# Dealing tokens to blocks by runs of 32, and two steps put elsewhere in the queues

## The chip, the cores and the metric

The kernel runs on one core of one Trainium2 chip. The metric is the device time of one execution in microseconds (us). "PE" is the TensorE matmul engine (PEld its weight load), DVE is VectorE, ACT is ScalarE, POOL is GpSimd, SP is SyncE, which here only issues DMAs.

## The reference

One layer of a decoder trunk over 512 tokens with 1024 channels, in float32: a SwiGLU feed-forward, a mixer (a gated linear recurrence beside attention in a window of 128 with sinks), and a second feed-forward. Each has a norm on its input and a norm on its output before the residual sum.

```python
def swiglu(x, w_gu, w_down):
    gate, up = jnp.split(x @ w_gu, 2, axis=-1)
    return (jax.nn.silu(gate) * up) @ w_down
...
x = x + 0.5 * rms_norm(swiglu(rms_norm(x, ffn1_pre_g[l]), ffn1_w_gu[l], ffn1_w_down[l]), ffn1_post_g[l])
y = hybrid_mixer(rms_norm(x, mix_pre_g[l]), ...)
x = x + rms_norm(y, mix_post_g[l])
x = x + 0.5 * rms_norm(swiglu(rms_norm(x, ffn2_pre_g[l]), ffn2_w_gu[l], ffn2_w_down[l]), ffn2_post_g[l])
```

The feed-forwards have 2816 hidden channels, 22 chunks of 128.

## The kernel before

**Arithmetic.** Every float32 operand of a product is split into a high part in PE's reduced float32 (`float32r`, rounded by a copy on ACT) and a low part (the rest, a subtraction on DVE). A product is three matmuls: high by high, high by low, low by high. For weights as for activations, DVE makes the low parts, and so PE waits for DVE where a low part is late.

**Seven products for eight.** In most groups the product of a 2x2 block matrix is made from seven block products instead of eight, with sums and differences of blocks on DVE ahead of them. The forms of the left operand are made by `Next.sums` and `Next.lows` (normed input, four calls for each feed-forward, kept for all groups of chunks). The hidden activations' forms for the down product are made by `seven_left` and `seven_right`: a11, s3, a12, s2, s4, a22, s1, in the order in which `seven_down` multiplies them.

**First feed-forward.** Chunks 0 to 3 are made by the plain path (`classic`) with a plain down product; then four groups of four chunks (4-7, 8-11, 12-15, 16-19) run in `octo`, and the last two chunks in `quad`. `octo` multiplies with tokens as the output's partitions, so the 512 tokens are dealt to four blocks of 128 (`NB` = 4). Block b gets tokens b, b + 4, b + 8 and so on: in `sums`, the product of x, gain and the inverse norm reads `xT` and `R` with a step of four words and writes a block as one run. The result of `octo` is turned back by DVE's 32x32 transposes (`turned`, line 934), which write `z` with a step of four words, so that `z` has the tokens in their natural order; `put` writes `z` to HBM by the queue of SP, and `fetch` brings it back with channels as partitions. `quad` with `dealt` set (the last pair of chunks) writes its high and low parts with the same step (lines 862 and 865).

While group g runs in `octo`, the forms of group g - 1 are made beside it (`seven_forms_of`), and after it `seven_down` makes the down product of g - 1, so there are three of these here, for chunks 4-7, 8-11 and 12-15. The second feed-forward has three `seven_down` too (chunks 6-9, 10-13, 14-17), with `quad` and no dealing.

**The order on the engines** is the order of the program: each engine has one queue, written out by hand. `W.take` hands out a weight tile and lets ACT and DVE split units ahead of it; a raw weight buffer whose units are all split is loaded anew. `hid.steps` is a list of small DVE and ACT steps, of which `seven_down` does one behind each product. In the first feed-forward the first of them has been done in `octo` already; so the steps stand one product earlier there than in the second.

**The residual stream.** `xT`, two tiles of 1 MB, lies in two of the five buffers for raw weights. In the first group, behind the down product's fourth chunk (c = 3), `lend` copies both tiles to HBM (POOL's queue, line 1305) and `W.load(2)` has SP load the next two raw weights into buffers that this frees. Later `give_back` fetches the stream. The down product's chunks are staged by ACT (line 1365) and put to HBM by POOL (line 1366).

**Tile buffers.** `wt` has 8 buffers and `t2k` 38; a new tile takes the buffer that was freed first, in program order, and waits for its last reader.

Of the kernel before, what the change touches and what calls it, by code (L numbers as in the profile page):

```python
# [12 lines left out]
ALU = mybir.AluOpType  # L13
AX = mybir.AxisListType

P = 128
T = 512
NB = T // P
# [101 lines left out]
def tile_layer(ctx: ExitStack, tc: tile.TileContext, out: bass.AP, **ins: bass.AP):  # L120
    nc = tc.nc
    pe, dve, act, pool, sync = nc.tensor, nc.vector, nc.scalar, nc.gpsimd, nc.sync
# [12 lines left out]
    HALF = [slice(0, T // 2), slice(T // 2, T)]  # L135
# [23 lines left out]
    def wt(name, w=T, dt=F32):  # L159
        return tmp.tile([P, w], dt, tag="w", name=name, bufs=NW)  # L160


    W = Weights()
# [378 lines left out]
    def stream():  # L542

        xs = [wpool.tile([P, 4 * T], F32, tag="raw", name=f"xT{i}", bufs=NRAW) for i in range(2)]
        return xs, [x[:, c * T:(c + 1) * T] for x in xs for c in range(4)]

    x_tiles, xT = stream()
# [8 lines left out]
    def x_low(x, src, gain, sl):  # L556
        dve.scalar_tensor_tensor(x[1][:, sl], src, gain, x[0].bitcast(F32)[:, sl], op0=ALU.mult, op1=ALU.subtract)

    class Next:


# [35 lines left out]
        def sums(self, k):  # L597


            n = f"{self.name}{k}"  # L600
            xa, xb, t13, t24 = (wt(f"{s}_{n}") for s in ("xa", "xb", "ta", "tb"))
            some = (lambda nm, dt: spare.pop() if spare else t2k(nm, dt)) if self.name != "a" else t2k
            if self.name != "a" and k < 2:
                spare.extend(fours(f"sums{k}", F32R))
            b11 = some(f"b11_{n}", F32R)
            highs = [some(f"{s}h_{n}", F32R) for s in ("b2", "t13", "t24")]
            l, r = HALF
            dealt = (lambda t: t.rearrange("p (t b) -> p b t", b=NB)) if self.dealt else lambda t: t
            for x, c in ((xa, k), (xb, k + 4)):
                dve.scalar_tensor_tensor(x.rearrange("p (b t) -> p b t", b=NB) if self.dealt else x, dealt(xT[c]), self.gain(c), dealt(self.R), op0=ALU.mult, op1=ALU.mult)  # L610
            act.copy(b11[:, l], xa[:, l])
            dve.tensor_sub(t13[:, l], xa[:, r], xa[:, l])
            dve.tensor_sub(t13[:, r], xb[:, r], xa[:, r])
            dve.tensor_sub(t24[:, l], xb[:, r], t13[:, l])
            dve.tensor_sub(t24[:, r], xb[:, l], t24[:, l])
            for h, x in zip(highs, (xb, t13, t24)):
                act.copy(h, x)
            self.made = n, xa, b11, highs, (xb, t13, t24)
# [147 lines left out]
    class Hidden:  # L766
# [45 lines left out]
        def seven_right(self, f, x, second):  # L812

            self.blocks[second, 1] = x
            a11, a21 = self.blocks[0, 0], self.blocks[0, 1]
            if not second:
                s3 = wt(f"s3{self.name}{f}")
                dve.tensor_sub(s3, a11, a21)
                self.form("s3", s3)
                return  # L820
            a12, a22 = self.blocks[1, 0], x
            s1, s2, s4 = (wt(f"{s}{self.name}{f}") for s in ("s1", "s2", "s4"))
            dve.tensor_sub(s1, a22, a21)
            dve.scalar_tensor_tensor(s2, s1, -1.0, a11, op0=ALU.mult, op1=ALU.subtract)

            for name, y in (("a22", a22), ("s1", s1), ("s2", s2)):
                W.later(1, self.high, name, y)

            def last_sum():
                dve.scalar_tensor_tensor(s4, s2, -1.0, a12, op0=ALU.mult, op1=ALU.subtract)  # L830
                self.high("s4", s4)
                self.low("s1")

            self.steps = [lambda: self.low("s2"), last_sum, lambda: self.low("s4"), lambda: self.low("a22")]

        def quad(self, f, last, ahead, seven_down=False, beside=lambda i: None):

            n = f"{self.name}{f}"
            l, r = HALF
            hs = None if seven_down else [(t2k(f"hh{n}{j}", F32R), t2k(f"hl{n}{j}", F32R)) for j in range(2)]  # L840

            def seven(b, form, first, ahead=AHEAD):
                hi, lo = W.take(ahead)
                for j in range(2):
                    o, js = b[:, HALF[j]], slice(j * P, (j + 1) * P)
                    for k in range(4):
                        xh, xl = self.nxt.t[form, k]
                        for i, (w, x) in enumerate(((hi, xh), (hi, xl), (lo, xh))):
                            pe.matmul(o, w[:, k, js], x, start=first and i + j + k == 0, stop=k == 3 and i == 2, skip_group_check=True)  # L849

            def low_parts(x, h):
                if seven_down:
                    (self.seven_right if h else self.seven_left)(f, x, last)
                    return
                def own(t):
                    return t.rearrange("p (t b) -> p b t", b=NB)[:, 2 * h:2 * h + 2] if self.nxt.dealt else t[:, HALF[h]]

                def like(t):
                    return t.rearrange("p (b t) -> p b t", b=2) if self.nxt.dealt else t

                for j in range(2):
                    act.copy(own(hs[j][0]), like(x[:, HALF[j]]))
                for j in range(2):
                    hh, hl = hs[j]
                    dve.tensor_sub(own(hl), like(x[:, HALF[j]]), own(hh.bitcast(F32)))  # L865

            def last_half():
                dve.tensor_mul(g1, g1, u4)

            A, D, B = (bank(f"{s}{n}") for s in "adb")  # L870
            p1, p7, u4 = (wt(f"{s}{n}") for s in ("p1", "p7", "u4"))
            u2, g1 = ((t2k if seven_down else wt)(f"{s}{n}") for s in ("u2", "g1"))
            seven(A, "b11", True)
            act.copy(B, A)
            seven(D, "t3", True)
            act.copy(p7, D)
            beside(1)
            seven(A, "t2", False)
            act.copy(u2, A)
            beside(2)  # L880
            seven(B, "b21", False)
            W.later(1, act.activation, p1, B, AF.Silu)
            beside(3)
            seven(A, "t1", False)
            act.copy(u4, A)
            beside(4)
            W.later(1, dve.tensor_add, u4, p7, u4)
            seven(D, "t4", False)
            dve.tensor_add(u2, u2, D)
            dve.tensor_mul(u2, p1, u2)  # L890
            W.later(1, low_parts, u2, 0)
            beside(5)
            seven(A, "b22", False, ahead)
            act.activation(g1, A, AF.Silu)
            if last:
                last_half()
                low_parts(g1, 1)
            else:
                W.later(1, last_half)
                W.later(2, low_parts, g1, 1)  # L900
            if not seven_down:
                for j in range(2):
                    self.hs[f + j] = hs[j]

        def octo(self, f, beside):


            n = f"{self.name}{f}"
# [22 lines left out]
            def turned(xs, h):  # L931

                for tb, x in enumerate(xs):
                    dve.transpose(z.rearrange("p (j n b) -> p b j n", n=32, b=NB)[:, 2 * h + tb], x.rearrange("p (j n) -> p j n", n=32))  # L934

                def put():
                    for i in range(4):
                        sync.dma_start(h_hbm[:, i * P:(i + 1) * P].rearrange("(j a) n -> a j n", a=32), z[32 * i:32 * (i + 1)].rearrange("p (j n) -> p j n", n=P))

                if h:  # L940
                    W.later(1, put)
# [4 lines left out]
            z = wide(f"z{n}")  # L946
# [355 lines left out]
    def lend(tiles):  # L1302

        for x, h in zip(tiles, xT_hbm):
            pool.dma_start(h, x)
# [9 lines left out]
    for g, (f0, f1) in enumerate(GROUPS1):  # L1315
# [18 lines left out]
        for c in range(KD):  # L1334
# [25 lines left out]
            b = pair_banks[c] if c < 2 else product(W.take(), xs, name=f"ya{g}{c}")  # L1360
            if g == 0 and c in (0, 1, 3, 4):
                (n1.sums if c in (0, 3) else n1.lows)(2 + c // 3)
            if g == 0:
                st = t2k("stage")
                act.activation(st, b, AF.Copy, scale=-1.0 if c >= KD // 2 else 1.0)
                pool.dma_start(in_hbm[c // 2][:, :, c % 2], in_halves(st))
                if c == 3:
                    lend(x_tiles)
                    W.load(2)
            else:  # L1370
                res.chunk(c, b, parts[c])

# [81 lines left out]
    for j in range(4):  # L1454
        b = in_product(f"pq{j}")
# [401 lines left out]
    for i in range(2):  # L1857
        x = wpool.tile([P, 2 * D], F32, tag="raw", name=f"x_rows{i}", bufs=NRAW)
# [82 lines left out]
```

## Time and profile before

| | us |
|---|---|
| median of 3 runs | 866.05 (864.41 to 869.21) |
| the profiled execution | 867.49 |
| its span, first to last instruction | 865.8 |
| PE busy | 850.1 |
| DVE busy | 717.8 |
| ACT busy | 520.1 |
| POOL busy | 212.1 |

In the profiled execution, group 4-7 begins in `octo` at 79 us; the three `seven_down` of the first feed-forward begin at 157, 221 and 280 us, those of the second at 659, 718 and 778 us. Times in rows are counted from the span's start. Matmuls are pipelined: one of 512 columns is shown as 0.39 us and the next starts 0.23 us later, so for PE a stretch's length between two products says more than the busy time of single rows.

### The profile page before, as it was taken

How to read it: one execution, taken by the hardware profiler on the slowest of the kernel's cores; microseconds unless marked ns; L12 is line 12 of the kernel's file. 1: busy time of each engine (PE TensorE's matmuls, PEld its weight loads, DVE VectorE, ACT ScalarE, POOL GpSimd, SP SyncE). 2: the span in 40 equal slices, each digit the busy share in tenths (PEclk: the TensorE clock that was granted, in tenths of full speed). 3: DMA queues.
4: the chain of work that ended last, by engine and by line, in shares of the span. 5: the costliest groups of instructions: out<-in, count | busy, mean ns of one | idle time of the engine just before them, and what ended most of it. 6: DMA issues, size and time to landing. Idle time of an engine off the chain costs nothing.

```text
span 865.8 us, 13808 instructions
## 1 busy us (share of the span) xinstructions
PE 850.1 (98%) x5252; PEld 764.0 (88%) x5252; DVE 717.8 (83%) x984; ACT 520.1 (60%) x871; POOL 212.1 (25%) x228
## 2 busy tenths in 40 slices
PE   9999999899999999999999999999999999999996
PEld 8988788798988998998788899888999998998995
DVE  4988898978979866889989589788789798889856
ACT  6645746476576565466888446444656666658552
POOL 2012000050230244344556045110201402303502
PEclk9999999999999999999999999999999999999999
DMA  7248419298396699322211140267733955938922
GB/s 245 75 149 291 161 55 309 72 240 279 81 254 212 137 254 328 109 69 78 98 50 50 49 137 11 65 144 229 263 97 103 235 156 132 234 98 184 261 91 97
DMA packets 118914, 133.85 MB, mean 155 GB/s; under 512 B 23152, under 2 KB 85952, under 8 KB 118336
## 3 DMA queue, kind: packets, MB, share of 16 engines
q1 hardware_dynamic: 103504, 98.23, 36.1%
q0 software_dynamic: 15200, 34.61, 17.9%
q8 instruction: 41, 0.67, 0.3%
q14 instruction: 25, 0.20, 0.1%
q10 hardware_dynamic: 144, 0.13, 0.0%
HBM read 96.25 MB, written 36.70 MB: 154 GB/s over the span
## 4 chain that ended last, share of the span: by engine, by line
PE 69%; DVE 15%; DMA 6%; issue 4%; ACT 4%; POOL 2%; SPq 1%; DVEq 0%; ACTq 0%; POOLq 0%
PE ab L849 11%; PE db L849 5%; PE aa L924 4%; PE bb L849 3%; PE da L924 2%; DMA raw_ad__3208<-in_ffn_w_down 2%; PE ba L924 2%; DVE za L934 2%; PE yb L1801 1%; PE yb L1800 1%; PE yb L1802 1%; PE wo L1755 1%; DMA raw_ayd__1426<-in_ffn_w_down 1%; DMA raw_ay__902<-in_ffn_w_gu 1%; PE yab L1824 1%
## 5 line engine op out<-in xcount | busy, mean ns | idle before, releaser
L1072 POOL DMA_DIRECT2D yp_a<-stage x42 | 36.3, 1053 | 188.3 <-ACT stage L1069 177.6
L1072 POOL DMA_DIRECT2D yp_b<-stage x42 | 36.8, 1145 | 148.8 <-ACT stage L1069 140.9
L480 PE MATMUL ya<-hla,whi_ad 128*128 128x512 f32 x62 | 24.2, 391 | 0.2 <-DVE hla L865 0.2
L479 PE MATMUL ya<-hha,whi_ad 128*128 128x512 f32 x62 | 24.1, 389 | 0.0
L481 PE MATMUL ya<-hha,wlo_ad 128*128 128x512 f32 x62 | 24.1, 389 | 0.0
L655 POOL TENSOR_TENSOR acca_r<-acca_r,sq_r 128x512 f32<-128x512 f32 x6 | 8.0, 1327 | 45.9 <-ACT sq_r L510 45.9
L1800 PE MATMUL yb<-whi_bd,hhb 128*128 128x512 f32 x48 | 18.7, 389 | 0.0
L1801 PE MATMUL yb<-wlo_bd,hhb 128*128 128x512 f32 x48 | 18.7, 389 | 0.0
L1802 PE MATMUL yb<-whi_bd,hlb 128*128 128x512 f32 x48 | 18.7, 389 | 0.0
L211 DVE TENSOR_TENSOR wlo_bd<-raw_bd,whi_bd 128x1024 fp32r<-128x1024 f32 x10 | 12.1, 1215 | 5.3 <-ACT whi_bd L206 5.3
L498 PE MATMUL an<-xh_mx,whi_xl 128*128 128x256 f32 x64 | 15.8, 287 | 0.0
L499 PE MATMUL an<-xh_mx,wlo_xl 128*128 128x256 f32 x64 | 15.5, 283 | 0.0
L782 POOL TENSOR_TENSOR usb<-usb,gsb 128x512 f32<-128x512 f32 x5 | 7.2, 1438 | 34.1 <-DVE usb L779 22.9
L1900 POOL TENSOR_TENSOR yp_b<-yp_b,grow 128x512 f32<-128x512 f32 x6 | 7.7, 1290 | 27.2 <-ACT ysq L1893 27.2
L479 PE MATMUL gt<-xh_mx,whi_gt 128*128 128x512 f32 x32 | 14.2, 444 | 0.0
L480 PEld LDWEIGHTS ya<-hla,whi_ad 128*128 128x128 f32 x62 | 11.6, 188 | 2.8 <-DVE hla L865 0.5
L479 PEld LDWEIGHTS ya<-hha,whi_ad 128*128 128x128 f32 x62 | 11.6, 188 | 2.5
L481 PEld LDWEIGHTS ya<-hha,wlo_ad 128*128 128x128 f32 x62 | 11.6, 188 | 2.4
L1801 PE MATMUL ybl<-wlo_bd,hhb 128*128 128x512 f32 (+1 forms) x36 | 13.2, 366 | 0.0
L1800 PE MATMUL ybl<-whi_bd,hhb 128*128 128x512 f32 (+1 forms) x36 | 13.2, 366 | 0.0
L1802 PE MATMUL ybl<-whi_bd,hlb 128*128 128x512 f32 (+1 forms) x36 | 13.2, 365 | 0.0
L1848 POOL DMA_DIRECT2D yp_b<-stage x8 | 4.4, 548 | 35.4 <-ACT stage L1847 35.0
(2157 smaller groups left out, 3737.7 us busy)
## 6 DMA issues: line engine op xcount, KB each, us to landing
yp_a<-stage POOLq DMA_DIRECT2D x50, 256.0 KB, 9.0
yp_b<-stage POOLq DMA_DIRECT2D x50, 256.0 KB, 8.1
h_a<-za SPq DMA_DIRECT2D x16, 256.0 KB, 4.2
hxa<-h_a SPq DMA_DIRECT2D x16, 256.0 KB, 19.4
raw_bd<-in_ffn_w_down SPq DMA_DIRECT2D x4, 1024.0 KB, 7.2
xn<-in_x SPq DMA_DIRECT2D x8, 256.0 KB, 5.6
xT_hbm<-xT POOLq DMA_DIRECT2D x2, 1024.0 KB, 5.7
yp_a<-yp_a SPq DMA_DIRECT2D x8, 256.0 KB
```

The lines of the kernel that those rows point to most:

```text
L479: pe.matmul(ps, hi[:, k, :], xh, start=start, stop=False)
L480: pe.matmul(ps, hi[:, k, :], xl, start=False, stop=False)
L481: pe.matmul(ps, lo[:, k, :], xh, start=False, stop=stop)
L498: pe.matmul(ps[:, sl], hi[:, k, :], xh, start=k == 0, stop=False)
L499: pe.matmul(ps[:, sl], lo[:, k, :], xh, start=False, stop=False)
L849: pe.matmul(o, w[:, k, js], x, start=first and i + j + k == 0, stop=k == 3 and i == 2, skip_group_check=True)
L924: pe.matmul(b[tb], x[:, blk], w[:, k, :], start=first and q + k + j == 0, stop=q + k == 2 and j == 2, skip_group_check=True)
L934: dve.transpose(z.rearrange("p (j n b) -> p b j n", n=32, b=NB)[:, 2 * h + tb], x.rearrange("p (j n) -> p j n", n=32))
L1072: pool.dma_start(o, st.rearrange("p (a b) -> p a b", a=2) if len(o.shape) == 3 else st, accum_op=ALU.add)
L1800: pe.matmul(ps, hh[:, blk], hi[:, k, cs], start=start, stop=False)
L1801: pe.matmul(ps, hh[:, blk], lo[:, k, cs], start=False, stop=False)
L1802: pe.matmul(ps, hl_[:, blk], hi[:, k, cs], start=False, stop=stop)
```

## The change

Three edits:

1. The tokens are dealt by runs of 32: block b gets tokens 32b to 32b + 31 of each 128. The view of the dealt order becomes "(i b n)" with n = 32. In `sums` one instruction over 512 becomes four over 128 each (`xT` and `R` are read as runs of 128; the output is written in four runs of 32). The transposes write runs of 32, and so do the casts and low parts in `quad`. `put` and `fetch` are as they were.
2. In `seven_right`, the low part of s1 (`self.low("s1")`) is no longer made with `last_sum`, but as a step of its own at the end of the list: behind the fourth product of `seven_down` in the first feed-forward and behind the fifth in the second, where it stood behind the first and the second. The seventh product is the one that reads it.
3. In the first group at c = 3, `lend(x_tiles)` and `W.load(2)` stand ahead of the staging of that chunk, not behind it.

```diff
+    def dealt(t):
+        return t.rearrange("p (i b n) -> p b i n", b=NB, n=32)
...
-            dealt = (lambda t: t.rearrange("p (t b) -> p b t", b=NB)) if self.dealt else lambda t: t
             for x, c in ((xa, k), (xb, k + 4)):
-                dve.scalar_tensor_tensor(x.rearrange("p (b t) -> p b t", b=NB) if self.dealt else x, dealt(xT[c]), self.gain(c), dealt(self.R), op0=ALU.mult, op1=ALU.mult)
+                if self.dealt:
+                    d = x.rearrange("p (b i n) -> p b i n", b=NB, n=32)
+                    for i in range(4):
+                        row = slice(i * P, (i + 1) * P)
+                        xi, ri = (t[:, row].rearrange("p (b n) -> p b n", b=NB) for t in (xT[c], self.R))
+                        dve.scalar_tensor_tensor(d[:, :, i], xi, self.gain(c), ri, op0=ALU.mult, op1=ALU.mult)
+                else:
+                    dve.scalar_tensor_tensor(x, xT[c], self.gain(c), self.R, op0=ALU.mult, op1=ALU.mult)
...
             def last_sum():
                 dve.scalar_tensor_tensor(s4, s2, -1.0, a12, op0=ALU.mult, op1=ALU.subtract)
                 self.high("s4", s4)
-                self.low("s1")
-
-            self.steps = [lambda: self.low("s2"), last_sum, lambda: self.low("s4"), lambda: self.low("a22")]
+
+            self.steps = [lambda: self.low("s2"), last_sum, lambda: self.low("s4"), lambda: self.low("a22"), lambda: self.low("s1")]
...
                 def own(t):
-                    return t.rearrange("p (t b) -> p b t", b=NB)[:, 2 * h:2 * h + 2] if self.nxt.dealt else t[:, HALF[h]]
+                    return dealt(t)[:, 2 * h:2 * h + 2] if self.nxt.dealt else t[:, HALF[h]]
 
                 def like(t):
-                    return t.rearrange("p (b t) -> p b t", b=2) if self.nxt.dealt else t
+                    return t.rearrange("p (b i n) -> p b i n", b=2, n=32) if self.nxt.dealt else t
...
-                    dve.transpose(z.rearrange("p (j n b) -> p b j n", n=32, b=NB)[:, 2 * h + tb], x.rearrange("p (j n) -> p j n", n=32))
+                    dve.transpose(z.rearrange("p (j b n) -> p b j n", n=32, b=NB)[:, 2 * h + tb], x.rearrange("p (j n) -> p j n", n=32))
...
+            if g == 0 and c == 3:
+                lend(x_tiles)
+                W.load(2)
             if g == 0:
                 st = t2k("stage")
                 act.activation(st, b, AF.Copy, scale=-1.0 if c >= KD // 2 else 1.0)
                 pool.dma_start(in_hbm[c // 2][:, :, c % 2], in_halves(st))
-                if c == 3:
-                    lend(x_tiles)
-                    W.load(2)
             else:
                 res.chunk(c, b, parts[c])
```

## The prediction

> **What bounds the kernel now.** I read the page's first part, then PE's waits, then PE's idle stretches by windows, and only then DVE's timeline ahead of each.
>
> ```profile
> span 865.8 us, 13808 instructions
> ...
> PE 850.1 (98%) x5252; PEld 764.0 (88%) x5252; DVE 717.8 (83%) x984; ACT 520.1 (60%) x871; POOL 212.1 (25%) x228
> ```
>
> PE is busy 850.1 of 865.8 us, so the change can win only from 15.7 us of idle and from matmuls that run slowly. PE's waits name the places:
>
> ```profile
> PE yea L1300 <- DVE hls L801: 3.9, 3, 2.4
> PE aa L924 <- ACT ba L929: 1.8, 1, 1.8
> ...
> PE yea L1300 <- ACT hhs L794: 0.6, 1, 0.6
> PE aa L849 <- ACT ba L874: 0.4, 1, 0.4
> ...
> PE po L1634 <- POOL pa L1621: 0.2, 1, 0.2
> ```
>
> The first four lie in the first feed-forward; the last, in the attention, is the longest one behind it. `yea` is the down product of s4, the fifth of seven, and it waits for DVE's low part of s4 in each of three groups; `aa` waits for a copy on ACT. In windows (us; PE, PEld, DVE, ACT, POOL busy; granted clock; DMA):
>
> ```profile
> 89.63:91.80 2.17, 0.39 (x2) 0.00 (x0) 1.45 (x2) 2.17 (x4) 0.00 (x0) 1.00 0.37 146
> 168.73:172.33 3.60, 0.54 (x3) 0.19 (x2) 3.60 (x6) 3.48 (x6) 0.18 (x1) 1.00 0.73 182
> 172.33:176.67 4.34, 4.34 (x23) 4.34 (x24) 4.26 (x5) 3.84 (x7) 4.05 (x6) 0.61 0.92 219
> 176.67:179.55 2.88, 2.88 (x27) 2.88 (x26) 1.77 (x2) 1.93 (x3) 1.12 (x3) 1.00 1.10 259
> 232.05:235.91 3.86, 3.13 (x26) 2.93 (x25) 3.82 (x5) 3.86 (x8) 2.86 (x4) 1.00 0.88 187
> 291.29:295.15 3.86, 3.14 (x27) 2.93 (x26) 3.86 (x6) 2.92 (x6) 2.86 (x4) 1.00 0.77 186
> ```
>
> A down product without a wait takes 2.88 us (fourth row). The s4 product of the first such group takes 3.60 + 4.34 = 7.94: 3.60 nearly without work, then 4.34 at a mean clock of 0.61, which costs 4.34 - 2.88 = 1.46 more. The second and third take 3.86, 0.98 too much each. With 1.8 idle at 89.63 that is 5.06 + 1.96 + 1.8 = 8.8 us that a faster DVE or an earlier load can reach.
>
> **The s4 wait: transposes and the moved step.** DVE ahead of it:
>
> ```profile
> 166.21 2.09 DVE L934 STREAM_TRANSPOSE za<-g1a 128x512 f32<-128x512 f32 x2
> 168.14 0.68 DVE L830 SCALAR_TENSOR_TENSOR s4a<-s2a,hxa 128x512 f32<-128x512 f32 x1
> 168.74 0.67 DVE L801 TENSOR_TENSOR hls<-s1a,hhs 128x512 fp32r<-128x512 f32 x1
> 169.33 1.21 DVE L318 TENSOR_TENSOR wlo_adt__1609<-raw_axd__1406,whi_adt__1608 128x1024 fp32r<-128x1024 f32 x1
> ...
> 171.59 0.68 DVE L801 TENSOR_TENSOR hls<-s4a,hhs 128x512 fp32r<-128x512 f32 x1
> ```
>
> DVE runs without a gap here, and what stands ahead of s4's low part (it ends at 172.27) delays PE one for one. The low part of s1 moves behind it: 169.33 - 168.74 = 0.6 gone. The transposes now write every fourth word and will write runs of 32 words. A pair takes 168.14 - 166.21 = 1.93. The same transpose with contiguous output is in the trace:
>
> ```profile
> 588.46 1.30 DVE L1810 STREAM_TRANSPOSE z<-xT 128x512 f32<-128x512 f32 x2
> 589.68 1.19 DVE L211 TENSOR_TENSOR wlo_bd<-raw_bd,whi_bd 128x1024 fp32r<-128x1024 f32 x1
> ```
>
> That is 1.22, so 0.7 less a pair. The new shape, runs of 32 with a hop of 512 bytes, is not in the trace. Bounds: no gain at all, or 0.7; a loss is the first rival. I take 0.7, since the nearest row with hops between runs, `COPY_PREDICATED` below (two runs of 128), costs no more than `TENSOR_TENSOR` on 256 contiguous elements:
>
> ```profile
> L1587 DVE COPY_PREDICATED sc<-up,sc 128x256 f32<-128x256 uint8 x12 | 5.0, 418 | 0.0
> L865 DVE TENSOR_TENSOR hlb<-g1b,hhb 128x256 fp32r<-128x256 f32 x4 | 1.5, 421 | 0.6 <-ACT hhb L862 0.6
> ```
>
> Four pairs lie on DVE's path between 113 and 168 us (two groups of chunks), two in each later group.
>
> **The earlier copy of the residual stream.** It is ordered behind the fourth down product's staging DMA on POOL's queue; the chain of waits runs through it:
>
> ```profile
> 66.70 2.19 POOL L1366 DMA_DIRECT2D yp_a<-stage  x3 [11.59 <-ACT stage L1365]
> 74.15 1.22 POOL L1305 DMA_DIRECT2D xT_hbm<-xT  x2
> ...
> 74.15 4.68 DMA xT_hbm<-xT
> 79.31 8.68 DMA raw_ay__902<-in_ffn_w_gu
> ...
> 88.01 1.23 DVE L292 TENSOR_TENSOR raw_ax__857<-raw_ay__902,raw_ax__857 128x1024 f32<-128x1024 f32 x1 [1.03 <-DMA raw_ay__902<-in_ffn_w_gu]
> ```
>
> The copy waits for no data (xT was written long before), so POOL can issue it at 66.70 + 2.19 = 68.9 instead of 74.15. The two loads (SP) that take the freed buffers follow, 5 us sooner less what the DMAs lose to each other. One landed at 88.0 and DVE had waited 1.03 for it: anything over 1.0 is slack. DVE's next step frees ACT's cast, ACT's copy `ba`, and PE; so 1.0 of the 1.8 at 89.63 goes and 0.8 stays, which is the ping-pong of DVE and ACT. The staging DMA that falls behind two copies on POOL is awaited by nobody before the last group. At nothing, then; uncovered it would cost about 1.2, POOL's time for the two.
>
> **The sums.** One product over 512 with step 4 becomes four over 128:
>
> ```profile
> 68.50 1.12 DVE L610 SCALAR_TENSOR_TENSOR xa_a<-xT,g,R_a 128x512 f32<-128x512 f32 x1
> 69.55 1.13 DVE L610 SCALAR_TENSOR_TENSOR xb_a<-xT,g,R_a 128x512 f32<-128x512 f32 x1
> ...
> 611.94 0.75 DVE L610 SCALAR_TENSOR_TENSOR xa_f<-xT,cols,R_f 128x512 f32<-128x512 f32 x1
> 612.60 0.75 DVE L610 SCALAR_TENSOR_TENSOR xb_f<-xT,cols,R_f 128x512 f32<-128x512 f32 x1
> ...
> L1437 DVE COPY home<-qT 128x128 f32<-128x128 f32 x4 | 1.7, 415 | 0.1
> ```
>
> Now 1.05 from start to start; contiguous 0.66. A low part over 512 takes 0.68, one over 256 (L865) 0.42, so 128 elements cost 0.13 and 512 cost 0.52; of the 0.66, 0.14 is fixed. A quarter then costs 0.27 and four 1.08: nothing won or lost. Bounds: 0.8 for four, if only 0.07 is fixed (the low part of s1 has 0.59 from start to start), and 1.66 by the 415 ns of a 128x128 copy. Four such products stand on DVE's path ahead of 88 us: from -1.0 to +2.4; I take 0, nearest to the rows of the same operation. [...]
>
> **The rest.** In the last pair of chunks, writes with step 4 become runs too:
>
> ```profile
> L862 ACT CAST hha<-u2a x2: 640/646/652, 323.9 to 324.4; 128x256 fp32r<-128x256 f32 x2
> L862 ACT CAST hhb<-u2b x4: 399/406/407, 815.7 to 836.0; 128x256 fp32r<-128x256 f32 x4
> ```
>
> 0.24 for each of four casts on ACT, as much on DVE; they stand before small waits of PE, of which I count 0.3. In the second feed-forward s1's low part moves too, and PE never waits there. It will follow DVE's L255 and stand before `wlo_br`, where DVE now idles 1.12:
>
> ```profile
> 673.34 1.23 DVE L255 TENSOR_TENSOR raw_bx__6699<-raw_by__6767,raw_bx__6699 128x1024 f32<-128x1024 f32 x1
> 675.68 1.23 DVE L250 TENSOR_TENSOR wlo_br__7049<-raw_bx__6699,whi_br__7048 128x1024 fp32r<-128x1024 f32 x1 [1.12 <-ACT whi_br__7048 L246]
> ...
> 675.59 0.39 PE L1826 MATMUL yab<-whi_bdv__6968,hls 128*128 128x512 f32 x1
> ```
>
> It would end near 673.34 + 1.23 + 0.67 = 675.2; PE needs it at 675.6. So nothing, with 0.4 to spare, in each of three groups. That cover gone (behind `wlo_br`, 675.68 + 1.23 + 0.67 = 677.6), PE would wait 2.0 in each, 6.0.
>
> **The sum.** At the first s4 product DVE is ready at 172.27 - 1.0 - 4 x 0.7 - 0.6 = 167.9; PE arrives at 168.73 - 1.0 + 0.12 (one of the product's 24 matmuls) = 167.85. So PE goes on at 167.9 instead of 172.3, 4.4 sooner, of which 1.0 is counted; the slow clock behind the wait, 1.46, goes with it: 3.4 + 1.5 = 4.9. The later groups: DVE's stage shortens by 1.4, PE's excess was 0.98; both go, 1.96, with 0.4 to spare. Late now is only DVE again, by tenths. Total 1.0 + 4.9 + 1.96 + 0.3 = 8.2 us. The profiled execution took 867.5 (span 865.8); minus 8.2 is 859.3. It lies 1.4 over the median of the three runs, 866.05, so I forecast 866.05 - 8.2 = 857.9.
>
> **Rivals.** First, slower: the hop of 512 bytes costs more than the step of 16, in the transposes. Each extra x on one transpose counts 16 times, less 1.6 from the copy and the moved step; it decides from x = 0.37 (4.3 lost, 0.5%), and at doubled transposes (x = 0.96) gives +13.8, 879.9. For it: no row has the shape. Against it: the row of L1587. [...] Chance 0.07. Second, the change doesn't do what it says, runs of 32 are no cheaper than now: DVE gains 1.6 only, the half clock and both 0.98 stay: 864.4. Chance 0.10. Third, the small products cost 0.415 each: DVE is 2.4 later at 88 us, the wait there grows by 1.4 instead of shrinking by 1.0, the s4 terms go all the same: 857.9 + 2.4 = 860.3. Chance 0.10. Fourth, s1's low part comes too late in the second feed-forward: 857.9 + 6.0 = 863.9. Chance 0.06. The forecast keeps 0.67.
>
> **Numbers.** 0.5%, 4.3 us, is about what a measurement of this kernel can tell from no change: the line lies at 861.7. Faster: 0.67 + 0.10 = 0.77. Within: 0.10 + 0.06 = 0.16. Slower: 0.07. The forecast's own range is 855.0 to 861: below, all 8.8 us of the waits, 1.0 from the small products and 0.6 from the last pair of chunks give 855.6, less as much again for the spread of the runs; above, the lower half of the terms. For 8 in 10 it reaches to the second and fourth rival: 855.0 to 864.5; what is left out is the first rival and a little on both ends.
>
> **What would show it.** L934 near 685 ns; DVE's s4 low part ahead of PE in all three groups; granted clock 1.00 from 160 to 180; the first xT copy issued near 69 and no DVE wait for `raw_ay`; PE's idle at the `ba` copy near 0.8; PE busy unchanged but for 1.5. Wrong if L934 stays above 1.0 us, if four L610 take over 1.3, or if PE waits for `hls` in the second feed-forward.

## The result and the profile after

| | median, us | lowest to highest | runs |
|---|---|---|---|
| before | 866.11 | 864.41 to 869.21 | 4 |
| after | 858.10 | 857.46 to 858.47 | 4 |

By the medians the change is faster by 8.0 us; the forecast was 857.9. The ratio is 0.9903 (95% interval 0.9874 to 0.9932); here and below, ratios are worked out from the single runs, and so they differ a little from the quotient of two medians. The profiled execution of after took 857.46 (span 855.8), against 867.49 before.

The page's first part, after:

```profile
span 855.8 us, 13837 instructions
...
PE 846.8 (99%) x5252; PEld 762.6 (89%) x5252; DVE 712.2 (83%) x1008; ACT 520.3 (61%) x871; POOL 210.8 (25%) x228
```

All of PE's waits that the view of waits lists for it:

```profile
PE warm L1155 <- POOL ident masks.py:199: 1.4, 1, 1.4
PE aa L933 <- ACT ba L938: 0.6, 1, 0.6
```

`warm` is the kernel's start. Every `yea` wait is gone, and of the wait at the copy `ba` 0.6 is left. Windows of the three s4 products (us; PE, PEld, DVE, ACT, POOL busy; granted clock; DMA):

```profile
166.87:169.75 2.88, 2.88 (x26) 2.88 (x25) 2.88 (x4) 2.88 (x5) 2.80 (x4) 1.00 0.88 169
...
225.13:228.01 2.88, 2.88 (x26) 2.88 (x25) 2.88 (x4) 2.88 (x6) 2.68 (x4) 1.00 0.82 156
283.39:286.27 2.88, 2.88 (x26) 2.88 (x25) 2.88 (x4) 1.47 (x3) 2.68 (x4) 1.00 0.66 143
```

The s4 products took 7.94, 3.86 and 3.86; now each takes 2.88, with the clock at 1.00. DVE ahead of the first, and the matmul that asks for its result:

```profile
161.18 1.30 DVE L943 STREAM_TRANSPOSE za<-g1a 128x512 f32<-128x512 f32 x2
162.40 0.65 DVE L840 SCALAR_TENSOR_TENSOR s4a<-s2a,hxa 128x512 f32<-128x512 f32 x1
162.97 1.21 DVE L318 TENSOR_TENSOR wlo_adt__1633<-raw_axd__1430,whi_adt__1632 128x1024 fp32r<-128x1024 f32 x1
164.69 1.22 DVE L318 TENSOR_TENSOR wlo_adu__1695<-raw_ayd__1450,whi_adu__1694 128x1024 fp32r<-128x1024 f32 x1 [0.51 <-ACT whi_adu__1694 L314]
165.83 0.68 DVE L811 TENSOR_TENSOR hls<-s4a,hhs 128x512 fp32r<-128x512 f32 x1
...
166.99 0.28 PE L1309 MATMUL yea<-hls,whi_adt__1632 128*128 128x256 f32 x1
```

A pair of transposes takes 162.40 - 161.18 = 1.22, as forecast. s4's low part ends at 166.51, 0.48 ahead of PE. But a new idle of 0.51 stands just where s1's low part was taken out; more on that below. The sums, the copy of the stream, and s1's low part in the second feed-forward:

```profile
60.82 1.13 DVE L618 SCALAR_TENSOR_TENSOR xa_a<-xT,g,R_a 128x128 f32<-128x128 f32 x4
61.87 1.14 DVE L618 SCALAR_TENSOR_TENSOR xb_a<-xT,g,R_a 128x128 f32<-128x128 f32 x4
...
67.98 1.24 POOL L1314 DMA_DIRECT2D xT_hbm<-xT  x2
...
75.83 1.60 SPq L171 DMA_DIRECT2D raw_ay__923<-in_ffn_w_gu  x2
...
86.15 1.22 DVE L292 TENSOR_TENSOR raw_ax__875<-raw_ay__923,raw_ax__875 128x1024 f32<-128x1024 f32 x1
...
664.44 0.68 DVE L811 TENSOR_TENSOR hls<-s1b,hhs 128x512 fp32r<-128x512 f32 x1
665.65 1.23 DVE L250 TENSOR_TENSOR wlo_br__7071<-raw_bx__6723,whi_br__7070 128x1024 fp32r<-128x1024 f32 x1 [0.52 <-ACT whi_br__7070 L246]
```

Four quarters take 61.87 - 60.82 = 1.05, what the one instruction took. POOL issues the copy at 67.98, not 74.15; SP issues the load that DVE had waited for at 75.83 (78.90 before), and DVE's step at 86.15 waits for nothing. In the second feed-forward s1's low part fills half of DVE's idle ahead of `wlo_br` and ends at 665.12; PE, which never waits there, asks for it at 665.56.

Where the time went: both traces have 5252 PE rows in the same order, so the start of the same matmul can be compared between the stages. By that, after is sooner by 0.72 at the start (no part of the change: profiles of one layout differ there by up to 0.6), 1.15 at the copy `ba`, 5.05 at the first s4 product, 0.99 and 0.97 at the other two, 0.91 at the last pair of chunks and 0.24 in the attention: 10.03. The medians differ by 8.0, because the profiled execution of before was 1.4 over its median and that of after 0.6 under.

### The profile page after: what moved, and what is told of

Read it like the earlier page. It is cut to its first block, busy times and chain, and to the rows that moved or that the text cites. A ratio compares the mean times of both kernels' runs of the same rounds, so it can differ in the third digit from the quotient of the medians.

```text
span 855.8 us, 13837 instructions
## 1 busy us (share of the span) xinstructions
PE 846.8 (99%) x5252; PEld 762.6 (89%) x5252; DVE 712.2 (83%) x1008; ACT 520.3 (61%) x871; POOL 210.8 (25%) x228
## 4 chain that ended last, share of the span: by engine, by line
PE 87%; DVE 6%; ACT 3%; POOL 1%; DMA 1%; issue 1%; SPq 0%; DVEq 0%; ACTq 0%; POOLq 0%
PE ab L858 11%; PE aa L933 10%; PE db L858 5%; PE da L933 4%; PE yaa L1309 3%; PE bb L858 3%; PE ba L933 3%; PE yda L1309 2%; PE aa L858 1%; PE yb L1811 1%; PE yb L1810 1%; PE yb L1809 1%; PE wo L1764 1%; PE yea L1309 1%; PE yba L1309 1%
```

## The experiments

The kernel before was timed beside each group of runs: 865.3, 865.98 and 865.88 us (57 runs, 863.1 to 870.0). Ratios are to it.

### One edit at a time

| kernel | us, median | ratio (95%) |
|---|---|---|
| edit 1 alone | 859.32 | 0.9923 (0.9902 to 0.9944) |
| edit 3 alone | 866.08 | 1.0003 (0.9989 to 1.0017) |
| edit 2 alone | 867.07 | 1.0010 (0.9996 to 1.0024) |
| all but edit 2 | 858.13 | 0.9909 (0.9891 to 0.9927) |

**Edit 1 alone**, runs of 32 in `sums`, `quad` and `turned`, all else as before:

```
-  dve.transpose(z.rearrange("p (j n b) -> p b j n", n=32, b=NB)[:, 2 * h + tb], ...)
+  dve.transpose(z.rearrange("p (j b n) -> p b j n", n=32, b=NB)[:, 2 * h + tb], ...)
```

> The kernel before with edit 1 alone (tokens dealt by runs of 32). The prediction's terms: the four pairs of transposes give 2.8 of the first s4 wait, the half clock behind it goes, groups 2 and 3 give 0.98 each, the copy wait of 1.8 stays at 88-90 us and s1's low part costs its 0.6: 8.2 - 1.0 - 0.6 = 6.6 us faster than before, about 859.5, with 0.6 of a wait left at the first s4 product. Revised theory (moving s1's low part is worth nothing, since DVE would wait for ACT's cast behind it anyhow; DVE also gains 1.1 to 1.3 from a load it no longer waits for): no s4 wait at all, 7.2 faster, about 858.9, provided that the load wait goes with this edit; if it belongs to edit 3, about 1 us of a wait is left at the first s4 product and 860. Rival (edit 1 is not what does it): less than 4 us.

6.0 us of the 8. No `yea` wait is in its trace: s4's low part is ready 0.6 ahead of PE, where the prediction's terms had 0.6 of a wait. What is left is the `ba` wait (view of waits):

```profile
PE aa L934 <- ACT ba L939: 2.3, 1, 2.3
```

with the load that DVE waits for ahead of it (timeline),

```profile
88.48 1.23 DVE L292 TENSOR_TENSOR raw_ax__875<-raw_ay__926,raw_ax__875 128x1024 f32<-128x1024 f32 x1 [1.60 <-DMA raw_ay__926<-in_ffn_w_gu]
```

and in this profile a half clock behind it (window; the clock is the third number from the end):

```profile
92.87:96.28 3.41, 3.41 (x10) 2.65 (x9) 3.41 (x4) 3.41 (x5) 0.00 (x0) 0.50 0.00 0
```

**Edit 3 alone**, `lend` and `W.load(2)` ahead of the staging:

> The kernel before with edit 3 alone (residual stream queued to HBM ahead of the staging). The prediction: DVE's wait of 1.03 for raw_ay at 88 goes, PE's wait at the ba copy falls from 1.8 to 0.8, the s4 waits and the half clock stay as they are, since DVE and PE both come 1.0 sooner: 1.0 faster. Rival: DVE gives the 1.0 back at its wait of 1.30 for the load raw_axd at 145 us, which does not come sooner; then the first s4 wait grows by as much and the time stays within 0.3 of before.

```profile
PE yea L1300 <- DVE hls L801: 3.9, 3, 2.4
...
PE aa L924 <- ACT ba L929: 0.7, 1, 0.7
```

From its waits: the `ba` wait fell by 1.1 and the s4 waits stayed, as forecast and not as the rival has it; but the time did not move (the interval's lower end is -0.95 us). In this trace PE's lead shrinks by 0.68 at the last pair of chunks, where ACT's cast waits for the weights `raw_ad`. Whether that load or the spread of the runs hides the 1.0 stays open. On top of edit 1 the edit shows: with edits 1 and 3 ("all but edit 2") the runs lie at 857.80 to 858.88, with edit 1 alone at 858.87 to 861.55.

**Edit 2 alone, and all but edit 2.** The edit is the move of one line:

```
                 self.high("s4", s4)
-                self.low("s1")
-            self.steps = [..., lambda: self.low("s4"), lambda: self.low("a22")]
+            self.steps = [..., lambda: self.low("s4"), lambda: self.low("a22"), lambda: self.low("s1")]
```

> The kernel before with edit 2 alone (s1's low part made later). The prediction: s4's low part is 0.6 sooner in each of three groups, so each s4 wait is 0.6 shorter: 1.8 us faster, the half clock stays or goes with it (a wait of 3.0 instead of 3.6). Revised theory: DVE gets to the low part of the weight unit adu 0.6 sooner, but that waits for ACT's cast of the unit, which stands behind ACT's cast of s4 and ended at 170.42 in the kernel before; so s4's low part comes 0.1 sooner at most and the time is 0 to 0.3 faster.

> The changed kernel without edit 2 (s1's low part back behind last_sum). The prediction counted 0.6 for it at the first s4 product with nothing to spare: 0.6 slower than the changed kernel (858.7). Revised theory: the 0.51 in which DVE waits for ACT's cast takes it up, s4's low part is 0.1 later and has 0.48 to spare: no difference from the changed kernel (858.1), no wait for hls in the trace.

Edit 2 makes no measurable difference either way, and the traces say why. ACT's cast `whi_adp` (the high part of a down weight) releases the stretch of DVE's work that ends with s4's low part; from the one to the other DVE has no other wait that matters. Edit 2 alone (first three rows) and all but edit 2 (next two); then ACT in the changed kernel (last two):

```profile
145.42 1.05 ACT L314 CAST whi_adp__1508<-raw_ayd__1426 128x1024 fp32r<-128x1024 f32 x1 [3.07 <-DMA raw_ayd__1426<-in_ffn_w_down]
169.19 1.23 DVE L318 TENSOR_TENSOR wlo_adu__1671<-raw_ayd__1426,whi_adu__1670 128x1024 fp32r<-128x1024 f32 x1 [0.51 <-ACT whi_adu__1670 L314]
170.33 0.68 DVE L801 TENSOR_TENSOR hls<-s4a,hhs 128x512 fp32r<-128x512 f32 x1
```

```profile
143.08 1.05 ACT L314 CAST whi_adp__1532<-raw_ayd__1450 128x1024 fp32r<-128x1024 f32 x1 [1.52 <-DMA raw_ayd__1450<-in_ffn_w_down]
166.55 0.68 DVE L811 TENSOR_TENSOR hls<-s4a,hhs 128x512 fp32r<-128x512 f32 x1
```

```profile
163.08 0.62 ACT L804 CAST hhs<-s4a 128x512 fp32r<-128x512 f32 x1 [4.03 <-DVE s4a L840]
163.61 1.05 ACT L314 CAST whi_adu__1694<-raw_ayd__1450 128x1024 fp32r<-128x1024 f32 x1
```

With edit 2 alone it is 170.33 - 145.42 = 24.91, the same as in the kernel before (rows below). Without edit 2 it is 23.47; in the changed kernel 23.46. DVE makes s1's low part in the very time in which it would wait for ACT: the cast of `adu` is queued behind ACT's cast of s4, which s4 itself releases.

### How DVE's time reaches PE

The prediction counted four pairs of transposes "on DVE's path between 113 and 168 us". But in the kernel before DVE waits near 147 for ACT's `hhs`, which is queued behind ACT's `whi_adp`, and that waits for a load. So the pairs of the first octo group (the last ends at 128.87) reach s4 along DVE's queue only as far as they outlast such waits. In the timelines, before (three rows) and after (five):

```profile
128.89 2.85 SPq L938 DMA_DIRECT2D h_a<-za  x4
...
146.68 1.05 ACT L314 CAST whi_adp__1508<-raw_ayd__1426 128x1024 fp32r<-128x1024 f32 x1 [3.74 <-DMA raw_ayd__1426<-in_ffn_w_down]
...
148.28 0.69 DVE L801 TENSOR_TENSOR hls<-s3a,hhs 128x512 fp32r<-128x512 f32 x1 [1.04 <-ACT hhs L794]
```

```profile
89.93 0.50 PE L933 MATMUL aa<-whi_ar__1000,t24h_a 128*128 128x512 f32 x1 [0.62 <-ACT ba L938]
...
125.76 2.85 SPq L947 DMA_DIRECT2D h_a<-za  x4
129.93 3.43 SPq L993 DMA_DIRECT2D hxa<-h_a  x4
...
134.42 1.21 SPq L171 DMA_DIRECT2D raw_ayd__1450<-in_ffn_w_down  x2
...
142.37 1.05 ACT L314 CAST whi_adp__1532<-raw_ayd__1450 128x1024 fp32r<-128x1024 f32 x1 [1.28 <-DMA raw_ayd__1450<-in_ffn_w_down]
```

They go another way: `put`, `fetch` and the loads of the down weights stand in SP's queue one behind the other, and ACT's cast waits for the last load. To test it, half of each transpose was done twice in the first octo group alone:

```
 dve.transpose(z...[:, 2 * h + tb], x.rearrange("p (j n) -> p j n", n=32))
+if f == CLASSIC1:
+    dve.transpose(z...[:, 2 * h + tb, :8], x.rearrange("p (j n) -> p j n", n=32)[:, :8])
```

> As the run before, but only in the first octo group (chunks 4-7), whose two pairs end at 126 us, far ahead of the first s4 product. Theory from the traces: these pairs count through SP's queue; the put of z, the fetch, and the loads of the down weights behind them go out 1.36 later, ACT's cast of the down unit and DVE's low part of s3 at 144 follow, and s4's low part comes 1.36 later against 0.48 to spare: 0.9 of a wait, 859.0, and no waits in groups 2 and 3. Rival (the prediction's plain count along DVE's queue, in which DVE's waits of 0.22 and 0.87 near 140 and 144 take up 1.09 and the spare 0.48 the rest): no wait, 858.1.

859.78 us (0.9928, 0.9910 to 0.9946). Rows of its timeline, and PE's wait at s4:

```profile
90.17 0.50 PE L933 MATMUL aa<-whi_ar__1000,t24h_a 128*128 128x512 f32 x1 [0.61 <-ACT ba L938]
...
127.81 2.85 SPq L949 DMA_DIRECT2D h_a<-za  x4
...
144.54 1.05 ACT L314 CAST whi_adp__1536<-raw_ayd__1454 128x1024 fp32r<-128x1024 f32 x1 [3.23 <-DMA raw_ayd__1454<-in_ffn_w_down]
```

```profile
PE yea L1311 <- DVE hls L811: 1.4, 1, 1.4
```

The changed kernel was also run once more, unchanged:

> The changed kernel once more, unchanged, as the measure for the next two on the same chip: 858.1, as before, with no wait for hls.

858.36 us (857.66 to 860.16 in six runs; 0.9904, 0.9882 to 0.9927). From its timeline:

```profile
90.57 0.50 PE L933 MATMUL aa<-whi_ar__1000,t24h_a 128*128 128x512 f32 x1 [0.64 <-ACT ba L938]
...
126.39 2.85 SPq L947 DMA_DIRECT2D h_a<-za  x4
...
144.39 1.05 ACT L314 CAST whi_adp__1532<-raw_ayd__1450 128x1024 fp32r<-128x1024 f32 x1 [2.67 <-DMA raw_ayd__1450<-in_ffn_w_down]
...
167.85 0.68 DVE L811 TENSOR_TENSOR hls<-s4a,hhs 128x512 fp32r<-128x512 f32 x1
```

Taken from the matmul with which PE goes on after the `ba` wait (91.80 before), in us:

| | before | after | half again in the first group | after, again |
|---|---|---|---|---|
| PE goes on to `put` on SP | 37.09 | 35.83 | 37.64 | 35.82 |
| `put` to the cast `whi_adp` | 17.79 | 16.61 | 16.73 | 18.00 |
| `whi_adp` to s4's low part | 24.91 | 23.46 | 23.46 | 23.46 |
| sum | 79.79 | 75.90 | 77.83 | 77.28 |

PE asks for s4's low part 77.06 after it goes on, and the instruction takes 0.68; so anything above 76.4 is a wait. The first line shows the first group's pairs: 1.26 sooner after, 1.81 later with the extra half transposes (0.45 each, not the 0.34 that was expected), and this 1.81 and 0.12 of the second line arrive at s4, where DVE's two waits in between should have taken up 1.09 by the prediction's count. PE waits 1.4 there, and the load was not late in this profile: the path by SP is shown. The third line shows the two pairs on DVE's own queue: 1.45. The second line is the load, and it has a spread of its own: 16.6 and 18.0 in the same kernel. In the second profile of the changed kernel, for which no wait was expected, that alone brings back 0.8 of the s4 wait.

**Half of each transpose twice, in all groups:**

> The changed kernel in which each transpose of the octo groups is followed by a second one of its first 256 columns (0.34 each, so a pair costs 1.97 again, as in the kernel before, with the new layout). If DVE's time for the transposes is what counted: s4's low part comes 4 x 0.68 = 2.7 later at the first s4 product against 0.48 to spare, so PE waits 2.2 there; 2 x 0.68 = 1.36 later in groups 2 and 3 against 0.6 to spare, so 0.75 in each: 3.7 slower than the changed kernel, 861.8, and up to 1.7 more where the wait brings a half-clock window. If it was the layout (what writes with step 4 does to others) and not DVE's time: no s4 wait and 858.1.

867.08 us (1.0012, 0.9999 to 1.0025): all of the gain gone, and 5 more than the 861.8 expected, 3.6 more than that with a half-clock window. Its waits, and a window:

```profile
PE yea L1310 <- DVE hls L811: 4.8, 3, 2.4
PE yea L1310 <- ACT hhs L804: 1.7, 1, 1.7
```

```profile
171.31:178.14 6.83, 6.04 (x28) 6.04 (x29) 6.48 (x8) 4.94 (x9) 5.24 (x6) 0.50 0.96 229
```

The layout was the new one and only DVE's time was back, so it is DVE's time that counts. How much of the gain it explains this run can't say to the microsecond: with the two halves a pair costs 1.22 + 0.90 = 2.12, more than the 1.93 of before. The waits are longer than expected since each half costs 0.45 and the load was late in this profile (17.9), and behind the wait of some 4.6 the clock was 0.50 for 6.83, two windows of 3.41 (row above).

### The shapes by themselves

Instructions were added behind the changed kernel's end, two of each:

> The changed kernel with some DVE instructions added behind its end that feed nothing, two of each: transposes and products (scalar_tensor_tensor) with different runs and hops, to time them by themselves; its own time is longer by about 22 us and says nothing. Expected for a 128x512 transpose: contiguous 0.68, runs of 32 with a hop 0.68, step 4 about 1.05. [...]

Rows of the timeline: three transposes, which write a run of 32 words in every 128, every fourth word, and every second word; then products that read runs of two words in every eight, every fourth word, and 128 contiguous words.

```profile
857.55 0.71 DVE L1950 STREAM_TRANSPOSE pr_z<-pr_src 128x512 f32<-128x512 f32 x1
...
859.42 1.08 DVE L1952 STREAM_TRANSPOSE pr_z<-pr_src 128x512 f32<-128x512 f32 x1
...
862.62 0.71 DVE L1956 STREAM_TRANSPOSE pr_z<-pr_src 128x512 f32<-128x512 f32 x1
...
873.34 0.75 DVE L1945 SCALAR_TENSOR_TENSOR pr_sink<-pr_in,pr_col 128x512 f32<-128x512 f32 x1
874.92 2.27 DVE L1945 SCALAR_TENSOR_TENSOR pr_sink<-pr_in,pr_col 128x512 f32<-128x512 f32 x2
...
879.53 0.74 DVE L1945 SCALAR_TENSOR_TENSOR pr_sink<-pr_src,pr_col 128x128 f32<-128x128 f32 x2
```

Runs of 32 cost 0.71, the same as contiguous (0.71 too); the first rival, a hop that costs more than the step, is void. Products with runs of 2, 4 and 32 words all took 0.75 like contiguous ones, and with step 4 1.12. So for these products runs of 32 are 16 times as long as the runs of two words that already took no more than contiguous ones (0.75 each).

A product over 128 columns took 0.35 alone, and 0.26 each from start to start in the kernel (1.05 for four), against the 0.27 (1.08 for four) that the prediction estimated.

### What is left, and a better version

The wait at `ba` that remains is ACT's order: the cast `whi_as` stands ahead of the copy. It was put behind it:

```
-                    hi, lo = W.take()
+                    hi, lo = W.take(AHEAD - 1 if f == CLASSIC1 and form == "b11" and q else AHEAD)
```

> The changed kernel with the second weight unit of the first octo product taken one unit less ahead, so that ACT's copy ba is queued in front of the cast whi_as and not behind it. If what is left of the wait at 89 us is ACT's order (the cast of 1.05, of which 0.95 from start to start, stands ahead of the copy): the copy starts at 88.35 instead of 89.30, PE's wait of 0.78 goes, 0.8 faster than the changed kernel, 857.3. Rival (the wait is DVE's and comes back at the next product, whose weight unit is now cast 1 us later): no difference, 858.1.

858.41 us (0.9903, 0.9887 to 0.9920): no measurable difference from the changed kernel. In its trace the `ba` wait is gone, by 0.87; but PE now comes to s4 as early as DVE, and 0.28 of it goes there.

So s4's low part was given more room, with edit 2 turned round: s1's low part goes back into DVE's idle time, and s4's follows at once, ahead of the weight units.

```
                 self.high("s4", s4)
+                self.low("s1")
+                self.low("s4")
-            self.steps = [..., lambda: self.low("s4"), lambda: self.low("a22"), lambda: self.low("s1")]
+            self.steps = [..., lambda: None, lambda: self.low("a22")]
```

> The changed kernel with ba ahead of the cast (as in the run b11_ahead) and with s4's low part made right behind s1's, in last_sum, ahead of the weight units adt and adu: DVE then uses its 0.51 of waiting, s4's low part is ready at about 164.4 and adt at 165.5, against 166.99 and 167.2 at which PE asks for them, so that 1.6 is to spare and not 0.48. If the 0.87 that b11_ahead gained at 89 us were lost for the reason that PE came to s4 before DVE (0.28 in its trace), all of it stays now: 0.8 faster than the changed kernel on the same chip, 857.3. Rival: b11_ahead gained nothing for another reason; then no difference.

857.28 us (0.9887, 0.9866 to 0.9908), 1.1 below the changed kernel on the same chip; all six runs (856.70 to 857.49) lie under all six of that one. DVE in its timeline:

```profile
162.52 0.65 DVE L840 SCALAR_TENSOR_TENSOR s4a<-s2a,hxa 128x512 f32<-128x512 f32 x1
163.09 0.68 DVE L811 TENSOR_TENSOR hls<-s1a,hhs 128x512 fp32r<-128x512 f32 x1
163.86 0.69 DVE L811 TENSOR_TENSOR hls<-s4a,hhs 128x512 fp32r<-128x512 f32 x1
```

s4's low part ends at 164.55, 2.0 after s4 was begun; in the changed kernel it ends 4.1 after (166.51 - 162.40). That is the best version of the study. A run with s4's low part early and `ba` as it was is missing, so how much each of the two moves gives is not shown. The same order in the old layout:

> The kernel before, old layout, with only s4's low part made right behind s1's in last_sum, ahead of the weight units. In the first group the low part of adt (its end moves from 170.5 to 171.3) becomes what PE waits for instead of s4's low part (172.27): 0.96 less; in groups 2 and 3 the 0.88 of each goes: together 2.7 faster than before, about 863, and up to 1.5 more where the shorter wait spares the half clock. Rival: DVE's time is what counts, whatever its order, and only the transposes help: no gain.

864.55 us (0.9975, 0.9957 to 0.9993): 1.3 faster, half of what was expected. `adt` takes the place of s4's low part in all three groups (1.0, 0.4 and 0.3 of PE's time), and in the third PE also waited 1.0 at a staging copy, which was not followed up.

## Why the prediction was right or wrong

**The sum** was right: 8.2 forecast, 8.0 by the medians. Its terms, by the starts of PE's matmuls in the two profiles:

| term | forecast | trace |
|---|---|---|
| copy `ba` | 1.0 | 1.15 |
| first s4 product | 4.9 | 5.05 |
| s4 in groups 2 and 3 | 1.96 | 1.96 |
| last pair of chunks | 0.3 | 0.91 |
| sums, second feed-forward | 0 | 0 |

The trace's terms make 9.1, for this pair of profiles. That the medians come within 0.2 of the forecast is in part luck: the 0.6 of s1's low part was not there, and what made up for it, a load that landed sooner and more time won at the last pair of chunks, varies from profile to profile by as much.

**First s4 product: right in size, wrong in its parts.** Of the DVE terms, 2.8 for four pairs measured 1.26 + 1.45 = 2.7, though two of the pairs get there by SP's queue and a load, not as "DVE runs without a gap" has it. The 0.6 for s1's low part was the failed step: it measured 0.0, because the step behind it waits for ACT. The prediction looked at what stood in DVE's queue and not at when ACT would release the next instruction. What filled the hole was 1.2 from a load that landed sooner in this profile. From `put` to `whi_adp` the four profiles in the old layout have 17.1 to 17.8, the nine in the new one 16.4 to 18.0; so no run ties the 1.2 to an edit, and whether the new layout helps the load on average stays open. Without it PE would have waited some 0.7 there, as it did 0.8 in the second profile.

**The half clock** went with the wait, as forecast: 0.61 before in the 4.34 behind it, 1.00 now.

**Groups 2 and 3** kept 0.6 to spare (forecast 0.4), and all 1.96 came.

**The copy of the stream** did at 88 us what was forecast, DVE's 1.03 gone and, of PE's wait of 1.8, 0.6 left (forecast 0.8). Alone it moved no time that could be measured.

**The sums** came out at 1.05 against 1.08: the fixed 0.14 from the rows of 256 and 512 columns held. The third rival (0.415 each) did not come.

**The last pair** was counted too small, 0.3 for 0.91; but in the second profile of the changed kernel 0.8 was lost there again, so this term has a spread as large as itself.

**PE's busy time** fell by 3.3, not by 1.5; the 1.8 beyond the half clock was not followed up.

## What to carry to other kernels

An instruction taken out of an engine's queue is worth only what the next instruction behind it can use (here 0.0 of 0.6, with 0.51 of waiting for ACT in its place): before counting it, look up when its other inputs are released. A delay can reach a stage by a queue that only issues transfers (a store, a fetch and loads in one line) although the engine itself waits in between (here 1.81 more on DVE in the first group, and PE waited 1.4 at s4). Where a rearranged layout is needed, short runs can be enough: here float32 products over 512 columns with runs of two words took DVE 0.75, as contiguous ones did, and with every fourth word 1.12.

## What the runs showed of the hardware

- **The half clock came in windows of 3.41 us, once behind an idle of 2.47 alone.** PE's idle is counted from the start of one matmul to the next, less the regular 0.23, or 0.12 with 256 columns. With edit 1 alone 2.47 (89.57 to 92.27) was followed by one window, clock 0.50 from 92.87 to 96.28. In the kernel before 0.79 and, one matmul later, 2.69 (169.52 to 172.33) were followed by one, 0.50 from 172.80 to 176.21. With half of each transpose twice in all groups 4.6 with one matmul in it came with two, 0.50 from 171.31 to 178.14. Idle of 1.94 (before, at the `ba` wait; clock 1.00 from 91.80 to 95.20) and of 1.52 (half again in the first group, PE's wait of 1.4 at s4; 1.00 from 168.80 to 171.50) was followed by none.
- **The spread of the kernel before goes largely with this clock.** Its 57 runs had a mean granted clock of 0.998 or more in 12 (mean 864.1 us), 0.996 in 23 (866.3) and 0.995 or less in 13 (868.2); the other 9, at 0.997, lie between the first two (865.4). One window is 0.5 x 3.41 / 866 = 0.002 of the clock. Read so, a wait like that at the first s4 product costs itself and, in some of the runs, one or two windows. Without it the times lie closer: 856.70 to 857.49 in the six runs of the best version, 863.1 to 870.0 in the 57 of before.
- **A 128x512 transpose that wrote every second word was as quick as a contiguous one** (0.71 each, in the rows behind the changed kernel's end); writing every fourth word took 1.08.
